# A fifteenth pair of chunks by seven products in the second layer's up-projection

## The chip, the cores and the metric

The kernel runs on one core of one Trainium2 chip. The core has a matrix engine (PE, with its weight loads listed apart as PEld), a vector engine (DVE), a scalar or activation engine (ACT), GpSimd (POOL), and a sync engine (SP) that here only issues transfers. Transfers can also be issued from the queues of ACT and POOL. All of them are served by the core's 16 DMA engines. The metric is the device time of one execution in microseconds (us); before the change it is 1697.43 us, the median of three runs (1696.9 to 1697.5).

## What is computed

Two sequences of 512 tokens, 1024 wide, go through a trunk of two layers in float32. Layer 0 mixes tokens with a Fourier transform, layer 1 with grouped-query attention; each layer then has an MLP with a squared ReLU, and a final norm ends it. What matters here is the MLP of layer 1:

```python
def sq_relu_mlp(h, w_up, w_down):
    a = jnp.maximum(h @ w_up, 0)      # 1024 -> 4096
    return (a * a) @ w_down           # 4096 -> 1024

x = x + sq_relu_mlp(rms_norm(x, mlp_norm[i]), mlp_w_up[i], mlp_w_down[i])
```

The change touches the first product, `h @ w_up`, for layer 1.

## The kernel before

**Number format.** Every operand of a product is split into two float32r halves, high and low, and one product of a 128x128 block of weights with a 128x512 block of activations is three matmuls: high by high, high by low, low by high (`product`, L863). A split is one cast on ACT (L82) and one subtraction on DVE (L83).

**Chunks and pairs.** The 4096 columns of `w_up` are 32 chunks of 128 columns. An ordinary chunk of one sequence takes 8 blocks of the inner dimension by 3 matmuls, which is 24 matmuls, and both sequences take 48. Most chunks are instead taken in pairs. A pair is two chunks, two sequences and two halves of the inner dimension, a product of 2x2 blocks, and it is computed with seven block products in place of eight (a scheme of Strassen and Winograd's kind). A block product is 4 inner blocks by 3 matmuls, 12 matmuls. So a pair takes 84 matmuls, and the same four chunk results done ordinarily take 96. Layer 0 has 16 pairs. Layer 1 has 14 pairs (chunks 0 to 27) and four ordinary chunks (28 to 31); `NPS` holds the two numbers.

**Operands.** `Blocks` makes the activation operands: b11 and b21 from the first sequence, b12 and b22 from the second, and the sums t1 to t4 of them. Each is four slots of the pool `act` (38 slots of 4 KB per partition, tag u4). The second sequence's operands and the sums are made by the generator `second` (L226, eleven steps), which is advanced step by step while the first sequence's products run. b12 is used by ordinary chunks alone.

**Leading pairs.** The products with b11 and b21 of the first `AHEADS[l]` pairs are made ahead, since these operands are there first: 8 pairs in layer 0, 6 in layer 1. A leading pair keeps a slot `t` with these two results until its remaining five products are made, and its weights are read a second time then (`load_sums`, L909). The ordinary chunks of the second sequence, `Regular(1, f)`, follow the leading pairs (L1064), between steps of `second`.

**The rest of each pair.** `rest` (L943) makes the remaining products in the order t2, t3, (for a pair that didn't lead: b21), t1, t4, b22, adds them up on DVE (L947, L951, L960, L969, L978), squares on ACT (L884, L885), and prepares the next pair's weight sums and splits between them. `out` (L982) then forms the sums that the second product needs as its operands, with four subtractions (L986 to L989, on POOL; for the last pair on DVE), and stores seven blocks of 256 KB to memory: three through the ACT queue (`spill_b`), four through SP (`spill_t`).

**The end of the stage.** While the last pair runs, the generator `ahead` (L1247) fetches and splits the first operands of the second product: b11, b21, t1, t3 during the pair, then t2, b22, t4, the first weights `w_row` and `w_sum`, and residuals from `park`. After the last pair come the ordinary chunks of the first sequence, `Regular(0, f)` (`last`, L1079 and L1113), and then the second product's first row (`Row`, weight `w`), and its sums (`Sums`, t1, t3, then t2, b22, t4). An ordinary chunk's result goes to `plain` through the ACT queue (L1008); the last MLP stage at the end of the kernel reads the four plain chunks back.

**Order.** A planner places the instructions of each engine, by its own estimate of times, in the order of the program's priorities. A `with tc.manual_schedule(...)` block keeps the named engines in program order. A slot is taken when its first writer is placed, and whoever takes it waits for the last reader of what it held. The pool of raw weights `rawp` has 5 buffers, that of split weights `wp` has 4, `tmp` 8.

```python
        for r in last:
            r.go()
```

Of the kernel before, what the change touches and what calls it, by code (L numbers as in the profile page):

```python
# [29 lines left out]
EPS = 1e-6  # L30
GRID_W = 64
ROPE_THETA = 10000.0
AHEADS = (8, 6)
NPS = (16, 14)
ROW, SUM = ("b11", "b21"), ("b22", "t1", "t2", "t3", "t4")
ROW_GROUPS = ((0, 4), (4, 4), (8, 4), (12, 4)), ((0, 4), (4, 4), (8, 4), (12, 2))
# [4 lines left out]
def trunk_kernel(ctx, tc, x_in, xt_in, y_out, dcos, dsin, feat, rope, gfour, gcol, grow, gfin,  # L41
                 w_four, w_nyq, w_qkv, w_o, w_up, w_row2, w_row4, w_sum2, w_sum4, w_down):
    nc = tc.nc
# [20 lines left out]
    def tm(shape=(P, 512), dt=F32):  # L64
        return tmp.tile(list(shape), dt, tag="t2", name=nm("t"))
# [4 lines left out]
    def ps():  # L70
        return psp.tile([P, 512], F32, tag="ps", name=nm("ps"))
# [30 lines left out]
    def halves(raw, n=512, home=own):  # L102
        hi, lo = home()
        split(hi[:, : 2 * n], lo[:, : 2 * n], raw)
        return [(hi[:, i * n : (i + 1) * n], lo[:, i * n : (i + 1) * n]) for i in range(2)]
# [740 lines left out]
    def project(q, fo, ws, parts, n=512):  # L846

        o, fs, x = ps(), slice(fo * P, (fo + 1) * P), xt(q, fo)
        for k in range(len(parts)):
# [10 lines left out]
    plain = [[drm.tile([P, 2, 512], F32, name=f"plain_{l}_{f}") for f in range(NF - 2 * NPS[l])]  # L860
             for l in range(2)]

    def product(o, w, h, first=True):  # L863

        n = len(h)
        for k in range(n):
            sl = slice(k * P, (k + 1) * P)
            for i, (x, y) in enumerate(((0, 0), (0, 1), (1, 0))):
                nc.tensor.matmul(o, w[x][:, sl], h[k][y], start=first and k + i == 0,  # L869
                                 stop=k == n - 1 and i == 2, skip_group_check=not first)  # L870

    def first_product(l, blocks, rows, ahead):
        def b(name):
            return [(h[0][:, i], h[1][:, i]) for h in blocks.b[name] for i in range(2)]

        def put(op, p, src, queue):
            for g, (p0, n) in enumerate(ROW_GROUPS[l] if op in ROW else SUM_GROUPS[l]):
                if p0 <= p < p0 + n:
                    (nc.scalar if op in ("b11", "b21", "b22") else queue).dma_start(spill[l][op][g][p - p0], src)

        np_, ah = NPS[l], AHEADS[l]

        def squares(t, src):
            nc.scalar.activation(t, src, AF.Relu)  # L884
            nc.scalar.activation(t, t, AF.Square)  # L885

        class Pair:
# [94 lines left out]
            def out(self, b11, b12, b21, b22, eng=nc.gpsimd, queue=nc.sync):  # L982
# [7 lines left out]
                for op, x in (("b11", b11), ("b21", b21), ("b22", b22), ("t1", t[:, 0]), ("t2", t[:, 1]),  # L990
                              ("t3", b12), ("t4", t4)):
                    put(op, p, x, queue)

        class Regular:


# [6 lines left out]
            def go(self):  # L1003
                q, w, o, t = self.q, halves(self.raw), ps(), tm()
                product(o, w[0], b("b11" if q == 0 else "b12"))
                product(o, w[1], b("b21" if q == 0 else "b22"), False)
                squares(t, o)
                nc.scalar.dma_start(plain[l][self.f - 2 * np_][:, q], t)  # L1008

            def run(self):  # L1010
                self.load()
# [3 lines left out]
        pairs = [Pair(p) for p in range(np_)]  # L1015
# [63 lines left out]
        last = [Regular(0, f) for f in range(2 * np_, NF)]  # L1079
        ahead = ahead(last[1:])  # L1080

        def early(ahead):

            pairs[-1].first()
            pairs[-1].second()
            pairs[-1].late = False
            for _ in range(3):
                yield next(ahead)

        for p, pair in enumerate(pairs[:-1]):  # L1090
            if p >= ah:
                pair.first()
            with tc.manual_schedule(engines={ET.DVE}) if p <= ah else nullcontext():
                done = pair.rest(pairs[p + 1], early(ahead) if not last and p == np_ - 2 else iter(()))
# [12 lines left out]
        with tc.manual_schedule(engines={ET.DVE, ET.SP} | (set() if last else {ET.PE})):  # L1107
            done = pairs[-1].rest(None, ahead)
        with tc.manual_schedule(engines={ET.SP}):
            for _ in ahead:  # L1110
                pass
            pairs[-1].out(*done, nc.vector)
        for r in last:  # L1113
            r.go()

    def second_product(l, blocks, rows, late=lambda split_them: None, ready=lambda m: None):
# [3 lines left out]
        def fetch(op, g, n):  # L1120

            h = []
            for k in range(0, n, 2):
                hi, lo = slot([P, 2, 512], F32R), slot([P, 2, 512], F32R)
                nc.sync.dma_start(f32(lo), spill[l][op][g][k : k + 2].rearrange("n p f -> p n f"))
                h.append((hi, lo))
            return h

        def put(op, h):
            for hi, lo in h:  # L1130
                split(hi, lo, f32(lo))
            b[op] = b.get(op, []) + [(hi[:, i], lo[:, i]) for hi, lo in h for i in range(2)]
# [11 lines left out]
        def residual(q, m):  # L1144
            if (q, m) not in there:
                xs[q, m] = slot([P, 2, 512], F32)
                nc.sync.dma_start(xs[q, m], park[q, m])
                there.add((q, m))
            return xs[q, m]
# [3 lines left out]
        def row_raw(m, g, n):  # L1153
            if (0, m, g) in early:
                return early[0, m, g]
            return load_raw(w_row4[4 * l + g, m] if n == 4 else w_row2[m], (P, 2, n * P))

        def sums_raw(m, g, n):
            if (1, m, g) in early:
                return early[1, m, g]  # L1160
            w = w_sum4[3 * l + g, m] if n == 4 else w_sum2[m]
            return [load_raw(w[:, i : i + 2], (P, 2, n * P)) for i in (0, 2)]
# [78 lines left out]
        def group(i, g, n, ops=(0, 5)):  # L1241
            ops = (("b11", "b21"), ("t1", "t3", "t2", "b22", "t4"))[i][slice(*ops)]
            for op in ops:
                b.pop(op, None)
                put(op, fetch(op, g, n))

        def ahead(regular):  # L1247
            n = SUM_GROUPS[l][0][1]
            if not regular:
                h = fetch("b11", 0, 4)  # L1250
                yield
                put("b11", h)
                h = fetch("b21", 0, 4)
                raws = [row_raw(0, 0, 4)]
                yield
                raws.append(row_raw(1, 0, 4))
                h1 = fetch("t1", 0, n)
                yield
                residual(0, 0)
                h3 = fetch("t3", 0, n)  # L1260
                yield
                put("b21", h)
                rows_early[0] = halves(raws[0], 4 * P)
                yield
                put("t1", h1)
                rows_early[1] = halves(raws[1], 4 * P)
                yield
                for m in range(2, 4):
                    early[0, m, 0] = row_raw(m, 0, 4)
                    residual(0, m - 1)  # L1270
                there_later.append(("t3", h3))
                for op in ("t2", "b22", "t4"):
                    there_later.append((op, fetch(op, 0, n)))
                    if op == "t2":
                        residual(0, 3)
                        early[1, 0, 0] = sums_raw(0, 0, n)
                residual(1, 0)
                return
            group(0, 0, ROW_GROUPS[l][0][1], (0, 1))
            regular[0].load()  # L1280
            yield
            group(0, 0, ROW_GROUPS[l][0][1], (1, 2))
            regular[1].load()
            yield
            group(1, 0, n, (0, 2))
            regular[2].load()
            yield
            group(1, 0, n, (2, 5))
            early[0, 0, 0] = row_raw(0, 0, ROW_GROUPS[l][0][1])
            for q in range(NSEQ):  # L1290
                residual(q, 0)
            early[1, 0, 0] = sums_raw(0, 0, n)
            for q in range(NSEQ):
                residual(q, 1)

        def finish(m):
            left[m] -= 1
            if left[m] == 0:
                nc.vector.tensor_add(xs[0, m][:, 1], xs[0, m][:, 1], e[m])
                nc.vector.tensor_add(xs[1, m], xs[1, m], e[m].unsqueeze(1).broadcast_to([P, 2, 512]))  # L1300
                ready(m)

        first_product(l, blocks, rows, ahead)
        e += [tm() for _ in range(4)]
        items, waiting = [], []
# [308 lines left out]
    for n in range(1, len(heads) + 1):  # L1614
        pts, nxt = [], []
        for t in range(NT):
# [3 lines left out]
            if n in (3, 5, 7, 9) and t == 0:  # L1620
                i = (n - 3) // 2
                rotate(raw[:, i * 256 : (i + 1) * 256].rearrange("p (h d) -> p h d", h=2), rt["q"], 2 + i // 2,
                       [late[i]], nc.gpsimd)
        last = nxt[-1] if nxt else last
# [8 lines left out]
        for i in {6: (0, 1), 8: (2,), 10: (3,)}.get(n, ()):  # L1633
            x = late[i].rearrange("p (h d) -> p h d", h=2)
# [94 lines left out]
    with tc.manual_schedule(engines={ET.PE, ET.Activation, ET.DVE, ET.Pool, ET.SP}):  # L1729
# [16 lines left out]
        x = xtok[0]  # L1746
# [196 lines left out]
```

## Time and profile before

| | |
|---|---|
| median of three runs | 1697.43 us |
| the profiled execution, its own time | 1697.05 us |
| its span, first to last instruction | 1695.3 us |
| granted TensorE clock | 0.999 |
| PE busy, matmuls | 1681.1 us, 7845 |
| DVE busy | 1231.3 us |
| ACT busy | 854.8 us |
| POOL busy | 334.6 us |
| leading pairs of layer 1's first product begin | about 1062 us |
| last pair of it ends, second product begins | 1350.64 us, about 1372.4 us |

The profile is one execution, with every instruction's start and duration, and what released it when its engine had been idle. A matmul's listed duration (about 390 ns) is longer than the distance to the next one, because matmuls overlap; lengths of PE work are therefore read from the start of one stretch to the start of the next. The profiled execution's own time is 1.75 us above its span and 0.38 us below the median.

### The profile page before, as it was taken

How to read it: one execution, taken by the hardware profiler on the slowest of the kernel's cores; microseconds unless marked ns; L12 is line 12 of the kernel's file. 1: busy time of each engine (PE TensorE's matmuls, PEld its weight loads, DVE VectorE, ACT ScalarE, POOL GpSimd, SP SyncE). 2: the span in 40 equal slices, each digit the busy share in tenths (PEclk: the TensorE clock that was granted, in tenths of full speed). 3: DMA queues.
4: the chain of work that ended last, by engine and by line, in shares of the span. 5: the costliest groups of instructions: out<-in, count | busy, mean ns of one | idle time of the engine just before them, and what ended most of it. 6: DMA issues, size and time to landing. Idle time of an engine off the chain costs nothing. (4 is left out here: it accounts for less than half of the span.)

```text
span 1695.3 us, 21868 instructions
## 1 busy us (share of the span) xinstructions
PE 1681.1 (99%) x7845; PEld 1395.1 (82%) x7845; DVE 1231.3 (73%) x1808; ACT 854.8 (50%) x1489; POOL 334.6 (20%) x304
## 2 busy tenths in 40 slices
PE   9999999999999999999999999999999999999998
PEld 7987888888788888888888888788888888888887
DVE  8788776557887879886588744687655479787864
ACT  7566444446243434467787714654444544344334
POOL 1321443221000000132344303014422200000002
PEclk9999999999999999999999999999999999999999
DMA  9643555449454545511000213335544686455322
GB/s 341 165 149 111 198 188 180 156 167 386 179 199 145 211 146 181 211 57 38 26 26 1 100 60 127 104 122 197 181 143 154 226 301 238 157 211 185 131 75 100
DMA packets 103679, 265.81 MB, mean 157 GB/s; under 512 B 10177, under 2 KB 10177, under 8 KB 103570
## 3 DMA queue, kind: packets, MB, share of 16 engines
q1 hardware_dynamic: 87266, 232.43, 39.0%
q10 hardware_dynamic: 14400, 26.22, 4.1%
q0 software_dynamic: 1904, 5.77, 1.7%
q8 instruction: 61, 1.00, 0.2%
q14 instruction: 48, 0.39, 0.1%
HBM read 189.40 MB, written 73.92 MB: 155 GB/s over the span
## 5 line engine op out<-in xcount | busy, mean ns | idle before, releaser
L869 PE MATMUL ps<-u,w 128*128 128x512 f32 x4656 | 1065.7, 389 | 3.4 <-DVE w L83 2.5
L869 PEld LDWEIGHTS ps<-u,w 128*128 128x128 f32 x4656 | 872.6, 188 | 187.9 <-DVE w L83 4.2
L82 ACT CAST w<-raw 128x1024 fp32r<-128x1024 f32 (+1 forms) x224 | 217.6, 981 | 442.3 <-PE ps L869 256.5
L83 DVE TENSOR_TENSOR w<-raw,w 128x1024 fp32r<-128x1024 f32 (+1 forms) x224 | 255.1, 1142 | 57.3 <-ACT w L82 56.7
L156 POOL TENSOR_TENSOR t<-t,t 128x512 f32<-128x512 f32 (+1 forms) x56 | 77.8, 1389 | 738.9 <-ACT t L154 683.0
L83 DVE TENSOR_TENSOR u<-u,u 128x1024 fp32r<-128x1024 f32 (+1 forms) x131 | 156.2, 1220 | 23.9 <-ACT u L82 23.3
L82 ACT CAST u<-u 128x1024 fp32r<-128x1024 f32 (+1 forms) x131 | 131.3, 1044 | 74.8 <-PE ps L869 47.8
L77 PE MATMUL ps<-u,u 128*128 128x512 f32 (+2 forms) x388 | 150.2, 388 | 0.4 <-DVE u L83 0.4
L1135 DVE TENSOR_TENSOR u<-ps,u 128x512 f32<-128x512 f32 x160 | 109.5, 686 | 53.5 <-PE ps L869 53.0
L79 PE MATMUL ps<-u,u 128*128 128x512 f32 (+2 forms) x388 | 144.4, 372 | 0.0
L78 PE MATMUL ps<-u,u 128*128 128x512 f32 (+2 forms) x388 | 144.2, 372 | 0.0
L869 PE MATMUL ps<-u,u 128*128 128x512 f32 x576 | 137.9, 390 | 0.6 <-DVE t L960 0.5
L869 PEld LDWEIGHTS ps<-u,u 128*128 128x128 f32 x576 | 107.8, 188 | 24.5 <-issue 0.9
L986 POOL TENSOR_TENSOR u<-u 128x512 f32<-128x512 f32 x28 | 37.2, 1328 | 401.0 <-ACT u L885 401.0
L83 DVE TENSOR_TENSOR u<-ps,u 128x512 fp32r<-128x512 f32 (+4 forms) x118 | 74.8, 650 | 19.5 <-ACT u L82 18.4
L79 PEld LDWEIGHTS ps<-u,u 128*128 128x128 f32 x388 | 73.1, 189 | 13.0
L77 PEld LDWEIGHTS ps<-u,u 128*128 128x128 f32 x388 | 73.3, 189 | 10.8 <-DVE u L83 0.6
L78 PEld LDWEIGHTS ps<-u,u 128*128 128x128 f32 x388 | 73.4, 189 | 10.4
L947 DVE TENSOR_TENSOR t<-ps,u 128x512 f32<-128x512 f32 x30 | 20.7, 691 | 80.6 <-PE ps L869 58.5
L82 ACT CAST u<-ps 128x512 fp32r<-128x512 f32 (+4 forms) x118 | 65.5, 561 | 27.3 <-PE ps L79 11.7
L852 DVE TENSOR_TENSOR u<-ps,u 128x512 f32<-128x512 f32 (+1 forms) x48 | 30.9, 644 | 64.4 <-PE ps L79 64.4
L77 PE MATMUL ps<-u,w 128*128 128x512 f32 (+2 forms) x192 | 65.0, 339 | 0.0
(247 smaller groups left out, 1986.9 us busy)
## 6 DMA issues: line engine op xcount, KB each, us to landing
raw<-w_up SPq DMA_DIRECT2D x82, 512.0 KB, 4.5
u<-spill_t SPq DMA_DIRECT2D x60, 512.0 KB, 6.2
raw<-w_sum SPq DMA_DIRECT2D x56, 512.0 KB, 4.1
u<-spill_b SPq DMA_DIRECT2D x45, 512.0 KB, 5.2
spill_t<-u SPq DMA_DIRECT2D x87, 256.0 KB, 2.0
spill_b<-t ACTq DMA_DIRECT2D x60, 256.0 KB, 3.1
raw<-w_row SPq DMA_DIRECT2D x28, 512.0 KB, 3.9
park<-u SPq DMA_DIRECT2D x24, 512.0 KB, 3.4
```

The costliest lines, as they stand in the source:

```text
L77: nc.tensor.matmul(out, lh, rh, start=first, stop=False)
L78: nc.tensor.matmul(out, lh, rl, start=False, stop=False)
L79: nc.tensor.matmul(out, ll, rh, start=False, stop=last)
L82: nc.scalar.copy(dst_hi, src)
L83: eng.tensor_sub(dst_lo, src, f32(dst_hi))
L156: nc.gpsimd.tensor_add(acc[q][:, :n], acc[q][:, :n], s[:, :n])
L852: nc.vector.tensor_add(x[:, :n], o[:, :n], x[:, :n])
L869: nc.tensor.matmul(o, w[x][:, sl], h[k][y], start=first and k + i == 0, stop=k == n - 1 and i == 2, skip_group_check=not first)
L947: nc.vector.tensor_add(u2, ob, t[:, 0])
L986: eng.tensor_sub(t[:, 0], b12, b11)
L1135: nc.vector.tensor_add(x, o, x)
```

## The change

`NPS[1]` stays 14 and sizes what the second product takes as pairs; the number of pairs of the first product is now `NPS[l] + l`, 15 in layer 1. The fifteenth pair is chunks 28 and 29; ordinary chunks are left for 30 and 31. The fifteenth pair is the last one and its results are stored plain, as the ordinary chunks were: four stores of 256 KB through SP, no subtractions. Pair 13, which was last, now goes through the ordinary `out` on POOL. In layer 1 eight pairs lead. `Regular` runs 2 chunks for each sequence in place of 4, and the steps of `second` that stood between four of them now stand between the two more leading pairs. In `ahead` two loads for ordinary chunks that no longer exist are gone.

```diff
-AHEADS = (8, 6)
+AHEADS = (8, 8)
 NPS = (16, 14)
...
-        np_, ah = NPS[l], AHEADS[l]
+        np_, ah = NPS[l] + l, AHEADS[l]
...
+            def out_plain(self, b11, b12, b21, b22):
+                for i, x in enumerate(((b11, b12), (b21, b22))):
+                    for q in range(2):
+                        nc.sync.dma_start(plain[l][i][:, q], x[q])
...
-                nc.scalar.dma_start(plain[l][self.f - 2 * np_][:, q], t)
+                nc.scalar.dma_start(plain[l][self.f - 2 * NPS[l]][:, q], t)
...
-            pairs[-1].out(*done, nc.vector)
+            if last:
+                pairs[-1].out_plain(*done)
+            else:
+                pairs[-1].out(*done, nc.vector)
...
             group(0, 0, ROW_GROUPS[l][0][1], (1, 2))
-            regular[1].load()
             yield
             group(1, 0, n, (0, 2))
-            regular[2].load()
             yield
```

## The prediction

> **What bounds the kernel now.** I read the page first, then the waits of PE, then the chain of waits, to see whether matmuls taken away shorten the span one for one.
>
> ```profile
> span 1695.3 us, 21868 instructions
> PE 1681.1 (99%) x7845; PEld 1395.1 (82%) x7845; DVE 1231.3 (73%) x1808; ACT 854.8 (50%) x1489; POOL 334.6 (20%) x304
> ...
> PE ps L869 <- DVE w L83: 2.5, 2, 1.5
> PE ps L356 <- POOL u L334: 1.8, 1, 1.8
> PE ps L869 <- DVE u L224: 0.9, 1, 0.9
> ...
> 1081.07 294.22 PE ps L869 x1296
> 1375.28 0.03 issue
> 1375.31 14.17 PE ps L869 x60
> ```
>
> The first two lines are the page's: PE is busy 99% of the span. The next three are the longest waits of PE (total, times, longest). The last three, from the chain of waits, are layer 1's first product from its second pair on: 1296 matmuls run without a gap from 1081.07 to 1375.28, that is 294.22 / 1296 = 0.227 us each. The only wait of PE in the touched stage is the 0.9 us before it is under way. So PE is the bound here, and it has nothing left to lose but matmuls: a matmul removed is worth 0.227 us as long as everything else still arrives in time, and anything late is a loss of its own.
>
> **What goes.** Before: 14 pairs of 84 matmuls and 8 ordinary products of 24, 1368. After: 15 of 84 and 4 of 24, 1356. Twelve fewer: 12 x 0.227 = **2.72 us**. All other engines are asked whether they keep up, in the two places where the cover changes. Let T be the start of pair 0's remaining products and E the end of the last pair.
>
> **The start, up to T.** The leading products are 6 x 24 + 4 x 24 = 240 matmuls before and 8 x 24 + 2 x 24 = 240 after, so T stays. The splits of weights are 10 either way, and the weight loads of the stage are 42 either way (two more second readings and two more for the pair, four fewer for ordinary chunks). b12 and b22 are needed first by an ordinary chunk: two leading pairs later, 48 matmuls or 10.9 us of ease. What is tight is DVE and, newly, the slots:
>
> ```profile
> 1100.00:1117.00 17.00, 17.00 (x77) 14.08 (x76) 16.84 (x17) 11.22 (x15) 0.00 (x0) 1.00 0.23 81
> 1117.00:1131.00 14.00, 14.00 (x63) 11.59 (x62) 12.22 (x16) 8.34 (x12) 0.00 (x0) 1.00 0.34 114
> ...
> 1116.84 1.22 DVE L83 TENSOR_TENSOR u<-u,u 128x1024 fp32r<-128x1024 f32 x1
> ...
> 1120.92 2.36 DVE L83 TENSOR_TENSOR u<-u,u 128x1024 fp32r<-128x1024 f32 x2
> ...
> 1127.60 2.88 PE L869 MATMUL ps<-u,u 128*128 128x512 f32 x12
> ```
>
> The first two rows are windows: length, then busy us of PE, PEld, DVE, ACT and POOL with their counts, the clock, the DMA engines' share and GB/s. DVE is busy 16.84 us of 17. The other rows are from the timelines. At 1127.60 pair 0 begins its b22 product (its weights are u tiles); four products of 12 x 0.227 lie ahead of it, so T = 1127.60 - 10.88 = 1116.72. The last two splits, t4, end at 1123.28, and the t4 product starts at T + 8.16 = 1124.88: 1.6 us to spare. After the change eight `t` slots are held, not six. Counting slots with the sums made as early as in this trace: b11, b21, b12, b22 and t2 hold 20, unsplit t1, t3, t4 six, the `t` eight, 34 of 38. Then t3 brings it to 36, half of t1 to 37, and the second half of t1 finds one slot and waits for b12, which is read last 2.72 us ahead of T. t1 is needed at T + 5.44, t4 at T + 8.16; three splits of 1.22 us after one cast of about 1 us from T - 2.72 end near T + 2. The bad end: all six splits and both sums wait for b12 and DVE does pair 0's own additions between them, 1.04 + 8 x 1.14 + 5 x 0.69 = 13.6 us from T - 2.72, which is 2.7 us after the t4 product's time. **Between 0 and 2.7 us; I take 0**, by the row of DVE at 1116.84, where a half of t1 is split at T already.
>
> **Between T and E.** Eight pairs have 60 matmuls left in place of six, seven have 84 in place of eight. Layer 0 already leads with eight, with seven operands of four slots and no b12, the same filling of the pool:
>
> ```profile
> 236.20 2.88 PE L869 MATMUL ps<-u,u 128*128 128x512 f32 x12
> 238.92 11.04 PE L869 MATMUL ps<-u,w 128*128 128x512 f32 x48
> 249.80 5.60 PE L869 MATMUL ps<-u,u 128*128 128x512 f32 x24
> 255.24 5.60 PE L869 MATMUL ps<-u,w 128*128 128x512 f32 x24
> ...
> 1131.00:1145.00 14.00, 14.00 (x63) 11.62 (x62) 10.66 (x13) 6.19 (x9) 6.33 (x4) 1.00 0.54 190
> ```
>
> These PE rows are layer 0's step from pairs that led to pairs that didn't (its first weights are lent slots, u): each stretch starts where the one before ends. In a short pair DVE is busy 10.66 us of 14 and the transfers 0.54. I cost this stretch at nothing, covered by PE. Pair 13's subtractions go from DVE to POOL,
>
> ```profile
> L986 POOL TENSOR_TENSOR u<-u x13: 1291/1294/2083, 1132.8 to 1334.1; 128x512 f32<-128x512 f32 x13
> L986 DVE TENSOR_TENSOR u<-u x1: 685/685/685, 1363.6 to 1363.6; 128x512 f32<-128x512 f32 x1
> ```
>
> 4 x 1.29 = 5.2 us of POOL, idle 80% of the span, and 4 x 0.69 = 2.7 us less DVE at the end. The added pair's 9 vector operations of 0.69 us lie within its 19 us.
>
> **The end, from E.** Here 96 matmuls (21.8 us) covered the fetching and splitting for the second product; now it is 48 (10.9 us). What they cover:
>
> ```profile
> 1350.64 24.64 PE L869 MATMUL ps<-u,w 128*128 128x512 f32 x108
> ...
> 1352.10 0.36 SPq L1125 DMA_DIRECT2D u<-spill_b  x1
> 1352.55 0.42 SPq L1125 DMA_DIRECT2D u<-spill_t  x1
> 1353.02 0.46 SPq L91 DMA_DIRECT2D raw<-w_row  x1
> 1354.69 1.03 SPq L1147 DMA_DIRECT2D u<-park  x2
> 1360.06 1.68 SPq L91 DMA_DIRECT2D raw<-w_sum  x2
> ...
> 1362.45 1.22 DVE L83 TENSOR_TENSOR w<-raw,w 128x1024 fp32r<-128x1024 f32 x1
> 1365.36 0.43 DVE L1202 TENSOR_TENSOR raw<-raw,raw 128x256 f32<-128x256 f32 x1 [1.09 <-DMA raw<-w_sum]
> 1367.51 0.42 DVE L1203 TENSOR_TENSOR raw<-raw,raw 128x256 f32<-128x256 f32 x1
> 1375.29 1.63 DVE L83 TENSOR_TENSOR u<-raw,u 128x512 fp32r<-128x512 f32 x3 [6.57 <-ACT u L82]
> ```
>
> E is 1350.64. The first row's weights are split by 1363.67 = E + 13.0; after the change they are needed at E + 10.9. The weights of its sums have landed by 1365.36 = E + 14.7, and need two sums, a cast and a split, some 2.2 us; they are needed at E + 10.9 + 2.7 = E + 13.6. So at unchanged times both are late: what counts is how much earlier the transfers get through.
>
> ```profile
> 1338.00:1342.00 4.00, 4.00 (x19) 3.33 (x18) 1.93 (x3) 0.00 (x0) 1.27 (x2) 1.00 0.70 226
> 1354.00:1358.00 4.00, 4.00 (x19) 3.30 (x19) 3.25 (x4) 2.91 (x4) 0.00 (x0) 1.00 1.06 408
> 1366.00:1370.00 4.00, 4.00 (x19) 3.30 (x19) 2.69 (x6) 0.60 (x1) 0.00 (x0) 1.00 1.03 399
> 1370.00:1374.00 4.00, 4.00 (x20) 3.30 (x19) 0.00 (x0) 1.40 (x3) 0.00 (x0) 1.00 0.55 182
> ...
> SPq L91 <- DMA spill_b<-t: 4.3, 1, 4.3
> SPq L1125 <- DMA spill_b<-u: 4.2, 1, 4.2
> ...
> 1339.71 0.39 SPq L1125 DMA_DIRECT2D u<-spill_b  x1
> ```
>
> The DMA engines are full, at about 400 GB/s, until 1370, and SP waited twice for the last pair's own stores (4.2 and 4.3 us). From 1339.71 = E - 10.9 to the landing of `w_sum` SP issues 12 transfers of 512 KB, two of `park` and two halves, with three stores of 256 KB from ACT: 16.5 x 0.524 MB = 8.6 MB, 21.6 us at 400 GB/s; it took 25 us, 3.6 us more. After the change two chunk loads are gone from that list and the three stores too (the plain ones stand behind the `park` loads in SP's order): 13 x 0.524 = 6.8 MB, 17.0 us, so `w_sum` lands between E + 6.1 and E + 9.7 and is split between E + 8.3 and E + 11.9, ahead of E + 13.6. By the same count `w_row`, 3 x 0.524 MB = 3.9 us less, lands 3.9 us earlier, is split at E + 9.1 and needed at E + 10.9. It fits, with some 1.7 us to spare. A cast placed behind the last ordinary chunk's squares on ACT already made the first sums' product a little late (12 matmuls in 3.29 us in place of 2.88, the split above at 1375.29); that 0.4 us stays in any case. For other small lateness I take **0.4 us** more; the bounds are 0 and, at unchanged times with DVE's 2.7 us of subtractions gone, E + 17.0 against E + 13.6, 3.4 us.
>
> [...]
>
> **Sum.** -2.72 + 0 + 0 + 0.4 = -2.3 us. On the profiled execution's own 1697.05 (its span and 1.75 us around it) that is 1694.7; the median stands 0.38 higher, so the forecast is **1695.1 us**, 0.14% below 1697.43. A measurement of this kernel can tell about 0.2%, 3.4 us, from no change, so this counts as no change.
>
> **Rivals**, in time of the median.
> - *The start is late*: a wait of PE for DVE's t1 or t4 split in pair 0, 0.5 to 2.7 us, leaves 0 to -2.2: 1695.2 to 1697.4, most likely 1696.4. For it: DVE at 16.84 of 17 us and a pool now filled to the last slot. Against it: 1.6 us to spare, and layer 0. Chance 0.17.
> - *The second product starts as late behind the last pair as before*, because SP again waits for some store: 3.4 us, or 5.0 if DVE is not freed in time, less 2.72. That is +0.7 to +2.3, **slower than before**: 1698.1 to 1699.7. It decides from `w_sum` landing later than E + 13.6 - 2.2 + 2.7 = E + 14.1. For it: the two rows of SP's waits. Against it: their stores have left. Chance 0.13.
> - *The whole queue of transfers must drain first*: full until 1370 = E + 19.4, less two loads (2.6 us) E + 16.8, plus 2.2 us of sums and splits: 5.4 us late, and the following sums' weights, next in the queue, up to 2 us more: +2.7 to +4.7, 1700.1 to 1702.1. Chance 0.06.
> - *More is gained than the matmuls*: the 0.9 us wait at the start and the 0.4 us at the end vanish too: -4.0, 1693.4. Only with another order by the planner. Chance 0.04.
>
> The forecast holds with 0.60, at 1694.3 to 1696.0. The range of 8 in 10 reaches over the first rival and part of the second: **1694.0 to 1699.0**. Faster by over 0.2% (below 1694.0) has 0.06, slower by over 0.2% (above 1700.8) 0.05, within it 0.89.
>
> **What would show it.** 12 matmuls fewer (7833); the same T; PE stretches of 0.227 us per matmul from T to E, which comes 480 + 588 - 1032 = 36 matmuls or 8.2 us later; 48 matmuls between E and the first row; the DMA share falling within some 12 us of E. A wait of PE on a u tile's split near 1117 to 1125 shows the first rival, on L83 near E + 11 to E + 14 the second and third. The forecast is wrong if PE waits more than 1.3 us in all in these two places, or if the planner's new order costs PE a wait elsewhere.

## The result, and the profile after

| | before | after |
|---|---|---|
| median | 1697.16 us (1696.72 to 1697.50, 4 runs) | 1715.8 us (1715.50 to 1716.04, 4 runs) |
| ratio, 95% interval | | 1.0107 [1.0095, 1.0118] |
| span of the profiled execution | 1695.3 us | 1714.3 us |
| granted TensorE clock | 0.999 | 0.995 |

The change made the kernel 18.6 us slower. The forecast was 1695.1 us with 1694.0 to 1699.0 as its range, so it was wrong, by far more than the range allowed. The page of the kernel after:

```profile
span 1714.3 us, 21868 instructions
PE 1686.6 (98%) x7833; PEld 1396.0 (81%) x7833; DVE 1238.1 (72%) x1813; ACT 856.2 (50%) x1490; POOL 342.6 (20%) x308
```

The 12 matmuls are gone (7833 for 7845), and yet PE is busy 5.5 us longer. So time was lost in two ways: PE stood still, and some matmuls ran slower. The longest waits of PE after (total, times, longest):

```profile
PE ps L869 <- DVE w L83: 5.3, 4, 2.6
PE ps L869 <- ACT w L82: 4.5, 1, 4.5
PE ps L869 <- DVE t L951: 3.4, 1, 3.4
PE ps L869 <- ACT u L82: 2.0, 2, 1.2
...
PE ps L869 <- DVE u L83: 1.0, 1, 1.0
```

Before, the touched stage had one wait, of 0.9 us. Where the new ones lie is seen in the timeline of PE after (start, length, count, and in brackets the wait ahead with what ended it):

```profile
1081.25 38.15 PE L869 MATMUL ps<-u,w 128*128 128x512 f32 x163
1120.16 7.14 PE L869 MATMUL ps<-u,w 128*128 128x512 f32 x29 [0.76 <-ACT u L82]
1130.68 4.57 PE L869 MATMUL ps<-u,w 128*128 128x512 f32 x12 [3.39 <-DVE t L951]
1135.05 2.95 PE L869 MATMUL ps<-u,u 128*128 128x512 f32 x12
...
1366.32 11.04 PE L869 MATMUL ps<-u,w 128*128 128x512 f32 x48
1381.89 1.22 PE L869 MATMUL ps<-u,w 128*128 128x512 f32 x2 [4.54 <-ACT w L82]
1383.34 4.58 PE L869 MATMUL ps<-u,w 128*128 128x512 f32 x10 [0.23 <-DVE w L83]
1389.11 3.29 PE L869 MATMUL ps<-u,u 128*128 128x512 f32 x12 [1.19 <-ACT u L82]
...
1402.06 5.29 PE L869 MATMUL ps<-u,u 128*128 128x512 f32 x22 [1.04 <-DVE u L83]
...
1434.85 5.31 PE L869 MATMUL ps<-u,w 128*128 128x512 f32 x15 [2.58 <-DVE w L83]
```

There are two places, the two that the prediction asked about. In the **lead**, the stretch of 204 matmuls up to pair 0's b22 product takes 1135.05 - 1081.25 = 53.8 us where it took 1127.60 - 1080.82 = 46.8 us: 7.0 us lost, 4.15 of them in the two waits. At the **end**, E is 1366.32; the second product begins at E + 15.6 in place of E + 10.9, and it waits four times more, 9.6 us in all.

The rest of the loss is the clock. Windows of the kernel after, each from about where PE resumes (length, busy us of PE, PEld, DVE, ACT, POOL with counts, granted clock, share of the DMA engines, GB/s):

```profile
1130.60:1134.60 4.00, 3.92 (x11) 3.12 (x12) 2.36 (x3) 3.05 (x4) 0.00 (x0) 0.64 0.02 4
1383.00:1387.00 4.00, 3.77 (x10) 2.88 (x10) 1.81 (x5) 0.00 (x0) 0.00 (x0) 0.50 0.57 214
1434.50:1438.50 4.00, 3.65 (x10) 2.87 (x11) 4.00 (x5) 0.49 (x1) 0.00 (x0) 0.63 0.89 326
```

After each of the three long waits (3.39, 4.54 and 2.58 us) the granted clock is 0.50 to 0.64 for some 4 us, and the ten matmuls from 1383.34 on take 4.58 us, twice 0.227 each. In the windows of 4 us that follow on these three it is 0.93, 0.91 and 0.95.

The account of the span, +19.0 us: 0.5 that already stands ahead of the stage (its first product after the 0.9 us wait starts at 1062.74, not 1062.28), 7.0 in the lead, -2.7 for the twelve matmuls, and the remaining 14.2 from E on, 9.6 of it waits. Of the 4.6 us that are left, about 4 are clock: the ten matmuls from 1383.34 and the fifteen from 1434.85 take 9.9 us where 25 x 0.227 would be 5.7. The 0.5 us lies within what executions differ by: a stretch of 24 matmuls behind it starts at 1074.88 before and at 1075.31 after, and in the profiles of the kernels below anywhere from 1074.72 (fifteen pairs, six leading) to 1075.88 (fourteen pairs, eight leading).

### The profile page after: what moved, and what is told of

Read it like the earlier page. It is cut to its first block, busy times and chain, and to the rows that moved or that the text cites. A ratio compares the mean times of both kernels' runs of the same rounds, so it can differ in the third digit from the quotient of the medians.

```text
span 1714.3 us, 21868 instructions
## 1 busy us (share of the span) xinstructions
PE 1686.6 (98%) x7833; PEld 1396.0 (81%) x7833; DVE 1238.1 (72%) x1813; ACT 856.2 (50%) x1490; POOL 342.6 (20%) x308
## 5 line engine op out<-in xcount | busy, mean ns | idle before, releaser
L83 DVE TENSOR_TENSOR u<-ps,u 128x512 fp32r<-128x512 f32 (+4 forms) x118 | 74.7, 649 | 19.6 <-ACT u L82 18.5
```

Of the source, the lines that this page charges most:

```text
L83: eng.tensor_sub(dst_lo, src, f32(dst_hi))
```

## Two causes, as the traces suggest them

**The lead.** In layer 1 one step of `second` is taken per leading pair from pair 4 on. A step's slots are taken in program order, so its casts come behind that leading pair's own copy (L903). Before, with six leading pairs, the steps after pair 5 had no such pair ahead of them. ScalarE's timeline before:

```profile
1092.82 0.58 ACT L903 COPY u<-ps 128x512 f32<-128x512 f32 x1
...
1093.28 2.95 ACT L82 CAST u<-u 128x1024 fp32r<-128x1024 f32 x3
```

and after:

```profile
1093.23 0.58 ACT L903 COPY u<-ps 128x512 f32<-128x512 f32 x1
...
1093.70 1.05 ACT L82 CAST u<-u 128x1024 fp32r<-128x1024 f32 x1
...
1098.92 0.58 ACT L903 COPY u<-ps 128x512 f32<-128x512 f32 x1
...
1099.39 1.05 ACT L82 CAST u<-u 128x1024 fp32r<-128x1024 f32 x1
...
1104.61 0.58 ACT L903 COPY u<-ps 128x512 f32<-128x512 f32 x1
...
1105.07 1.05 ACT L82 CAST u<-u 128x1024 fp32r<-128x1024 f32 x1
```

Three casts in a row have become one per leading pair, 5.7 us apart. The sums that need them (L240 is the first of t1) start 9.5 us later. The line L240 before, with its first and last start:

```profile
L240 DVE TENSOR_TENSOR u<-u,u x2: 1218/1218/1218, 1097.8 to 1104.8; 128x1024 f32<-128x1024 f32 x2
```

and after:

```profile
L240 DVE TENSOR_TENSOR u<-u,u x2: 1217/1218/1220, 1107.3 to 1113.1; 128x1024 f32<-128x1024 f32 x2
```

From there on DVE has no pause (windows after):

```profile
1110.00:1120.00 10.00, 9.40 (x42) 7.45 (x40) 10.00 (x10) 5.69 (x8) 0.00 (x0) 1.00 0.14 52
1120.00:1130.00 10.00, 7.14 (x29) 5.29 (x29) 9.97 (x12) 5.48 (x7) 0.00 (x0) 1.00 0.38 131
```

**The end.** The first row's weights had landed in time: the load of `w_row`, issued at 1363.83, took 9.3 us (issue table after: KB, us to landing).

```profile
raw<-w_row SPq DMA_DIRECT2D x1, 512.0 KB, 9.3
```

That is E + 6.8, and PE wants the split at E + 10.9. But ScalarE's timeline after reads

```profile
1377.39 0.60 ACT L884 ACTIVATE t<-ps 128x512 f32<-128x512 f32 x1 [1.67 <-PE ps L869]
1377.89 1.04 ACT L82 CAST u<-u 128x1024 fp32r<-128x1024 f32 x1
...
1379.85 1.04 ACT L82 CAST u<-u 128x1024 fp32r<-128x1024 f32 x1 [0.40 <-ACT t L885]
1380.80 1.04 ACT L82 CAST w<-raw 128x1024 fp32r<-128x1024 f32 x1
```

while before it read

```profile
1359.09 2.00 ACT L82 CAST u<-u 128x1024 fp32r<-128x1024 f32 x2
1360.99 1.05 ACT L82 CAST w<-raw 128x1024 fp32r<-128x1024 f32 x1
1361.93 1.07 ACT L884 ACTIVATE t<-ps 128x512 f32<-128x512 f32 x2
```

The order is turned round. The cast of the row's weights, and two casts of operands, now stand behind the squares (L884) of the last ordinary chunk. Those can only start when PE has finished that chunk, which is the moment at which PE itself wants the weights. The wait of 1.19 us one product later looks the same: the casts for the first sums stand behind the copy that ends the first row (L1147), which waits for PE. ScalarE's timeline after:

```profile
1387.96 0.59 ACT L1147 COPY t<-ps 128x512 f32<-128x512 f32 x1 [6.12 <-PE ps L869]
1388.44 1.45 ACT L82 CAST u<-raw 128x512 fp32r<-128x512 f32 x3
```

A second suspect was SP: it waited 5.9 and 8.7 us for plain stores (waits of SP's queue after).

```profile
SPq L91 <- DMA plain<-t: 8.7, 1, 8.7
...
SPq L997 <- DMA plain<-t: 5.9, 1, 5.9
```

## The experiments

All ratios are to the kernel before, with 95% intervals. They were measured in three groups, each with the kernel before beside it: its median was 1697.1 us beside the two steps, the six leading pairs, the first sequence's plain stores and the row's split; 1697.6 us beside the kernel before with eight leading pairs, all final plain stores, the cover given back and all cures; 1697.7 us beside the last two. The changed kernel's 1715.8 us was measured beside 1697.2, so differences between groups carry some 0.5 us.

### Two steps per leading pair

```diff
-                for _ in range(3 - 2 * l):
+                for _ in range(2 * (p < 7) if l else 3):
```

> The changed kernel, but leading pairs 4, 5 and 6 advance the operand generator by two steps each and pair 7 by none (in the changed kernel each of 4 to 7 advances it by one). Theory A (steps pinned): slots are taken in program order, so each step's first cast cannot be placed before the first copy of the leading pair that stands ahead of it; one step for each pair leaves DVE idle about 9 us before T, and the work that is left over makes PE wait 0.76 and 3.39 us at pair 0 with about 2.8 us more at a reduced clock. Then here these two waits go and the time falls by 5 to 7 us from 1715.8, to about 1709 to 1711; the waits at the end of the stage stay. Rival B (slots): eight held result slots leave too few for t1, t3 and t4 until b12 is read. Then taking the steps earlier fills the pool earlier and nothing is gained: 1714 to 1718, with the wait near 1120 to 1130 still there.

Measured: 1709.54 us, 1.0072 [1.0057, 1.0087], 6.3 us below the changed kernel. PE's timeline has one stretch:

```profile
1081.55 47.64 PE L869 MATMUL ps<-u,w 128*128 128x512 f32 x204
```

Both waits in the lead are gone, and the waits of the end are what they were (4.5, 1.2, 1.0 and 2.6 us). The eight leading pairs hold their slots of the pool `act` as in the changed kernel, so it was not the size of the pool that made the steps late.

### Fifteen pairs, six of them leading

```diff
-AHEADS = (8, 8)
+AHEADS = (8, 6)
```

> The changed kernel, fifteen pairs, but six leading pairs as before the change. Leading work is 192 matmuls in place of 240, so the remaining products of pair 0 begin 10.9 us earlier. Theory A: the steps run as early as before the change, yet DVE (busy 16.8 of 17 us in that stretch before the change) has 10.9 us less for them; PE waits some 6 to 9 us at pair 0, most of it at full or half clock, and the whole is at or above the changed kernel: 1714 to 1722. Rival B (slots): with six held slots nothing waits for slots, PE waits 0 to 3 us at pair 0, and the time falls to about 1708 to 1711. Both: the end of the stage loses what it loses in the changed kernel (about 14 us with what follows in the second product).

Measured: 1715.73 us, 1.0111 [1.0094, 1.0128]. The lead loses as much as with eight, in another way: the steps come as early as before (L240 at 1097.6), but 48 matmuls fewer stand ahead of pair 0's b22 product, which begins at 1123.72, 43.1 us after the stretch's start at 1080.65 in place of 156 x 0.227 = 35.4 us. Its listed waits are 3.1 us (1.50, 0.45, 0.41, 0.74), and the granted clock from 1100 to 1120 is 0.83. Right behind the first three waits, which lie within four microseconds with one matmul between each two, 28 matmuls take 9.29 us (from 1110.84) where 28 x 0.227 would be 6.4.

### The kernel before with eight leading pairs

Fourteen pairs and four ordinary chunks, `AHEADS = (8, 8)`, nothing else.

> The kernel before (fourteen pairs, four ordinary chunks) with eight leading pairs instead of six, nothing else. Pinned-steps theory: the steps still stand one behind each of the pairs 4 to 7, so they come as late as in the changed kernel, and the lead loses as it does there in place of T's matmuls: DVE t and ACT u waits of 2 to 6 us, 1699 to 1705. Rival (it is the number of pairs, not the lead, that makes the lead late): no wait in the lead, 1696.5 to 1697.5. In both, no 4.5 us wait before the second product.

Measured: 1697.83 us, 1.0 [0.9991, 1.001]. The first theory of this expectation falls as it was put: the steps are as late as in the changed kernel, and still nothing waits. PE's timeline of this kernel, and the line L240:

```profile
1081.82 58.24 PE L869 MATMUL ps<-u,w 128*128 128x512 f32 x252
```

```profile
L240 DVE TENSOR_TENSOR u<-u,u x2: 1219/1220/1221, 1107.8 to 1113.6; 128x1024 f32<-128x1024 f32 x2
```

I had overlooked that with four ordinary chunks two more leading pairs also mean 48 more matmuls before pair 0 needs its sums. What decides is the time between the first t1 sum and pair 0's b22 product. Worked out for each kernel as matmuls x 0.227 less the start of L240 (both from the stretch's first matmul), beside what the stretch really took:

| kernel | matmuls | first L240 after | time left then | stretch without waits | stretch taken |
|---|---|---|---|---|---|
| before | 204 | 17.0 us | 29.3 us | 46.3 us | 46.8 us |
| changed | 204 | 26.0 us | 20.3 us | 46.3 us | 53.8 us |
| two steps per pair | 204 | 18.4 us | 27.9 us | 46.3 us | 47.5 us |
| 15 pairs, 6 lead | 156 | 17.0 us | 18.5 us | 35.4 us | 43.1 us |
| 14 pairs, 8 lead | 252 | 26.0 us | 31.2 us | 57.2 us | 58.1 us |

With 27.9 us or more the lead loses no more than 1.2 us; with 20.3 and 18.5 us it loses 7.5 and 7.7, so that b22 is reached 27.8 and 26.1 us after the first sum. So the chain of sums, casts and splits seems to need about that long; this is worked out from the table, not measured by itself. The changed kernel took both ends of the slack: fifteen pairs leave two ordinary chunks fewer as cover, and two more leading pairs, with a step pinned to each, use the time that they give back.

### The first sequence's plain stores on POOL's queue

```diff
-                nc.scalar.dma_start(plain[l][self.f - 2 * NPS[l]][:, q], t)
+                (nc.scalar if q else nc.gpsimd).dma_start(plain[l][self.f - 2 * NPS[l]][:, q], t)
```

The line issues the stores of chunks 30 and 31 for the first sequence, two in all.

> The changed kernel, but the plain stores of the first sequence's two ordinary chunks are issued from POOL's queue, not ACT's. Theory C (order on ACT): the first row's weights are cast only behind the squares of the last ordinary chunk, which wait for PE, so the wait of 4.5 us (and the clock lost after it) stays; only the second half of the first sums' weights, which stood behind the landing of one such store for 8.7 us, comes earlier, and 1 to 3 us are gained: 1713 to 1715. Theory D (order of transfers): this hold of SP's queue is what makes the second product late; then the waits from 4.5 us on vanish or halve and 8 to 12 us are gained: 1704 to 1708. If transfers are limited by bandwidth alone, nothing changes: 1715 to 1717.

Measured: 1714.07 us, 1.01 [1.0085, 1.0115], 1.7 us below the changed kernel. The long wait shrinks from 4.54 to 3.23 us and the others stay (1.19, 1.04, 2.58). Without the issues of the stores between squares and casts (0.33 us each in the changed kernel) ScalarE is through a little sooner: PE, which waits for the row's cast, resumes at 1380.14, E + 14.3, in place of E + 15.6. With all final plain stores on POOL's queue, further down, SP's queue waits for no plain store any more (5.9 and 8.7 us in the changed kernel), and yet this wait is 3.23 us there too. So that hold was not what made the second product late.

### The row's split ahead of the last squares

The split of row 0 is issued inside `ahead`, as soon as its load is, the split of the ordinary chunks' weights ahead of all, and ScalarE keeps program order there:

```diff
+            rows_early[0] = halves(early[0, 0, 0], 4 * P)
...
-        with tc.manual_schedule(engines={ET.SP}):
+        for r in last:
+            r.prep()
+        with tc.manual_schedule(engines={ET.SP} | ({ET.Activation} if last else set())):
...
-        for r in last:
-            r.go()
+            for r in last:
+                r.go()
```

> The changed kernel with ACT held in program order at the end of the stage: the weights of the two last ordinary chunks are split first, then the operands t2, b22, t4 and the first row's weights (split here, not in the second product), and the squares of the ordinary chunks come behind them. The stores stay where they were. Theory C (order on ACT): the first row's weights landed 6.8 us behind the last pair's end and are split by some 9 us behind it, so the wait of 4.5 us before the second product goes, and with it the 10 matmuls at half clock: 5 to 8 us gained, 1708 to 1711. Theory D (order of transfers): the first sums' weights still land late and PE waits 3 to 5 us one product later, so at most 2 us are gained: 1714 to 1716.

Measured: 1709.58 us, 1.0073 [1.0058, 1.0088], 6.2 us below the changed kernel. ScalarE's timeline of this kernel:

```profile
1375.93 1.04 ACT L82 CAST w<-raw 128x1024 fp32r<-128x1024 f32 x1
1376.88 0.58 ACT L884 ACTIVATE t<-ps 128x512 f32<-128x512 f32 x1
```

and PE's:

```profile
1378.65 2.56 PE L869 MATMUL ps<-u,w 128*128 128x512 f32 x10 [0.90 <-DVE w L83]
```

No transfer was taken away, only orders were changed, ScalarE's above all, and of the 4.54 us 0.90 is left; the ten matmuls take 2.56 us, not 4.58. So the long wait was order, not transfer. The waits further in (1.19, 1.04, 2.57) stay.

### All final plain stores on POOL's queue

Both kinds of plain store are issued by POOL (the line of `Regular` as above, and L997 with `nc.gpsimd`). These are the six stores at the end of the stage; the expectation's "eight" counts the second sequence's two, which stay on the ACT queue and are issued long before.

> The changed kernel with all eight last plain stores on the POOL queue and no change of order. If the 1.0 and 2.6 us waits later in the second product are the loads that SP issues late because it stands behind the plain stores' transfers (5.9 and 8.7 us in the changed kernel), both go, and with 1.7 us that the first ordinary chunk's store alone gave: 1709 to 1713. If they stem from the late start of the second product's splits on ScalarE and VectorE, only the 1.7 us come again: 1713 to 1715.

Measured: 1711.75 us, 1.0082 [1.0065, 1.0099], 4.1 us below the changed kernel. The 4.54 us wait is 3.23 us, as with the first sequence's stores alone; the 1.04 us wait goes, the 2.58 us one only falls to 2.0, and 1.19 stays. So the stores on SP's queue may cost some 2 to 3 us beyond those of ScalarE's; the two intervals overlap, so the size of it is not shown. The last wait has another cause.

### The cover given back

The products of the last ordinary chunks of the first sequence are made twice, which leaves the output as it is:

```diff
-                product(o, w[0], b("b11" if q == 0 else "b12"))
-                product(o, w[1], b("b21" if q == 0 else "b22"), False)
+                for _ in range(2 - q):
+                    product(o, w[0], b("b11" if q == 0 else "b12"))
+                    product(o, w[1], b("b21" if q == 0 else "b22"), False)
```

The expectation's "48 more matmuls" is the sum over both chunks, 24 for each.

> The changed kernel in which the first product of each of the two last ordinary chunks is made twice over, so that 48 more matmuls (10.9 us) stand before each and the output is the same. Cover theory: waits before and in the second product (4.5, 1.2, 1.0, 2.6 us) and the half clock go, some 9 to 14 us, against 10.9 us of added work: 1712 to 1718. Order theory alone: the 4.5 us wait stays nearly whole, since the split still stands behind the squares of the last ordinary chunk, and only the later waits go: 1718 to 1724.

Measured: 1715.84 us, 1.0108 [1.0092, 1.0123], as long as the changed kernel: 48 matmuls more, 10.9 us, and 10.9 us of waits and slow clock less. PE's timeline of this kernel:

```profile
1365.72 24.64 PE L869 MATMUL ps<-u,w 128*128 128x512 f32 x108
...
1434.18 26.20 PE L869 MATMUL ps<-u,w 128*128 128x512 f32 x108 [2.57 <-DVE w L83]
```

With 96 matmuls behind E, as before the change, the first waits of the end (4.54, 0.23, 1.19 and 1.04 us) are gone. This does not separate cover from order, as I had wanted, because the planner also put the casts ahead of the last squares again; the kernel with all cures, next, does separate them. But the last wait, 2.57 us, stays with all the cover given back.

### All cures together

Two steps per leading pair, all plain stores on POOL, ScalarE's order at the end, and the casts of the first sums ahead of the copy that ends the first row.

> The changed kernel with both cures together and two more of the same kind: two steps of the second product's loads, sums and splits per leading pair; the ordinary chunk's split ahead of the last ordinary chunk's squares on ScalarE; all eight last plain stores on the POOL queue, so that no transfer of SP's waits for one of them; and the casts of the second product's first sums ahead of the copy that ends its first row group. Order theory (every wait of the changed kernel is one of instruction order, and the half clock follows from the waits): all four waits of the end (4.5, 1.2, 1.0, 2.6 us) and both of the lead go, and the time is that of before less 12 matmuls, 1694.4 us, 1694 to 1698. Rival, cover theory (with two ordinary chunks there are 48 matmuls fewer between the last pair and the second product, so what is cured at its start comes back behind it): the two waits at the start go, but 1.0 and 2.6 us stay or grow and the clock falls there again, 1700 to 1704, about what the two cures give when added (1715.8 - 6.2 - 6.2 = 1703.4).

Measured: 1699.76 us, 1.0012 [1.0003, 1.0021], between the two expectations, and 3.6 us less than the two main cures added. The cover is as small as in the changed kernel, 48 matmuls, and still the waits of 4.54, 1.19 and 1.04 us are gone, but for 0.90 us ahead of the row's second half. So the smaller cover alone did not make them: with the orders and queues mended it is enough. One other wait is left:

```profile
1418.50 41.82 PE L869 MATMUL ps<-u,w 128*128 128x512 f32 x183 [2.42 <-DVE w L83]
```

This is the split of the t3 operand of the fifth set of summed weights. The window of the same kernel ahead of it shows DVE without a pause:

```profile
1410.00:1418.00 8.00, 6.08 (x27) 4.69 (x25) 8.00 (x11) 7.67 (x9) 0.00 (x0) 1.00 0.97 358
```

Before the change this same split was just in time. PE's and DVE's timelines before:

```profile
1411.40 48.96 PE L869 MATMUL ps<-u,w 128*128 128x512 f32 x214
```

```profile
1416.19 1.21 DVE L83 TENSOR_TENSOR w<-raw,w 128x1024 fp32r<-128x1024 f32 x1
```

It ended at 1417.4, and the 26 matmuls ahead of its product ended at 1411.40 + 26 x 0.227 = 1417.3. There was nothing to spare, so PE could be earlier there only if DVE was.

### That split moved ahead, and some work of DVE left out

Both start from the kernel with all cures. In the first the fifth sums' t3 operand is split right behind their t1 and t2 operands:

```diff
-                if k:
+                if k and not (l and k == 4):
                     sums.split_3()
...
                         nsums.split_12()
+                        if l and k == 3:
+                            nsums.split_3()
```

> The version with all cures, and the split of the fifth sums' t3 operand issued right behind that of its t1 and t2 operands, ahead of the t4 operand's (layer 1 alone). In the version with all cures TensorE waits once more, 2.4 us for that split, at a time when VectorE is busy without a gap (10.00 of 10 us). If it is VectorE's order alone, the split comes about 2.4 us earlier (two splits of 1.22 us and one of 0.69 stand behind it now), the wait shrinks to 0 to 1.2 us (the operand's other half is next), and the time is 1699.8 less 1 to 2.4, 1697.3 to 1699. If VectorE's work is the bound there whatever its order, the wait goes over to the u split that is now behind it, and the time stays 1699 to 1700.5.

Measured: 1696.06 us, 0.9991 [0.9982, 0.9999]. PE's timeline of this kernel:

```profile
1372.84 2.54 PE L869 MATMUL ps<-u,w 128*128 128x512 f32 x10 [0.90 <-DVE w L83]
...
1419.06 41.32 PE L869 MATMUL ps<-u,w 128*128 128x512 f32 x181 [0.16 <-DVE t L1150]
```

The wait of 2.42 us has become 0.16, and the time fell by 3.7 us, more than the wait, to below the expected range. The runs of the kernel with all cures lay between 1697.9 and 1700.9 us, and its profiled one was among the shortest. Most of the longer ones show a granted clock of 0.998 over the whole run, the three shortest 0.999, so a slower clock behind the same wait may be the rest; no trace of a longer run is kept. In the second kernel the three sums of weights (`sum_123`) are left out for that set, so its output is another one.

> The version with all cures, in which the three sums of layer 1's fifth set of summed weights (1.8 to 2.1 us of VectorE) are left out, so the output changes. If the last 2.4 us wait is VectorE being full from about 1402 us on, it shrinks by about what is left out, to 0 to 0.7 us, and the time to 1697.5 to 1698.5. If the operand's load or its cast comes too late whatever VectorE does, the wait stays at 2 us or more and the time at 1699 to 1700.5.

Measured: 1696.74 us, 0.9998 [0.9988, 1.0007]. PE's timeline of this kernel:

```profile
1417.11 43.13 PE L869 MATMUL ps<-u,w 128*128 128x512 f32 x189 [1.01 <-DVE w L83]
```

The wait falls by 1.4 us where some 1.8 were left out, less than expected (0 to 0.7 us were to be left). So what the wait ends with is VectorE's work, its amount here and its order in the kernel above, not the load or the cast.

## Why the prediction was wrong

**"What goes" was right.** Twelve matmuls are 2.7 us. The kernel with all cures and the moved split fits it: 1694.5 us of span, 0.8 less than before, with 1.1 us of waits left in the second product and 0.6 us of later start and 0.6 us of longer lead that before does not have. -2.7 + 1.1 + 0.6 + 0.6 = -0.4, and it measures -0.8.

**"Between T and E" was right.** From pair 0's b22 product to E are 1366.32 - 1135.05 = 231.3 us after and 1350.64 - 1127.60 = 223.0 before, 8.2 us more, as worked out. POOL took the subtractions without a wait of PE.

**"The start, up to T" failed.** The sentence that failed is "counting slots with the sums made as early as in this trace". The number of matmuls ahead of T stayed 240 as computed, and the slots were not the trouble. But the steps that make the sums are tied one by one to leading pairs, so with two more of them the sums began 9.5 us later. The slack was read from the old trace (1.6 us), as if the feeding work stood where it had stood. The term was taken at 0, with 2.7 as its bad end; 7.0 came. The rival *The start is late* named the right place and the right engine, and was sized by the wrong cause.

**"The end" failed in its order, more than in its transfers.** `w_row` was to land 3.9 us sooner than before behind E; before, it landed at 1353.02 + 7.1 = E + 9.5 (7.1 us to landing in the issue table), after, at E + 6.8, 2.7 us sooner, early enough for the split at E + 9.1 that I had written down. But the cast began at E + 14.5. The prediction had seen the pattern ("a cast placed behind the last ordinary chunk's squares on ACT") and gave it 0.4 us "in any case". That was its price with 96 matmuls of cover, when only the sums' casts stood there. With 48 the planner set three more casts, the row's among them, behind the same squares, and the price was 4.5 us. "It fits, with some 1.7 us to spare" was a sum over transfers that left out the queue in which the next instruction stands. The rival *The second product starts as late behind the last pair as before* was right in sign and place; it looked for a store that SP waits for. That was a part of it, some 4 us at the most (all final stores on POOL), and 0.7 to 2.3 us was too small. The sum over transfers missed it as well: the second half of `w_sum`, forecast to land by E + 9.7, was issued at 1376.9, when SP's wait of 8.7 us was over, and landed 2.6 us later, at E + 13.2. VectorE came to it only at 1383.20, behind the row's late split, so that this lateness was hidden behind ScalarE's.

**Two terms were missing.** The sum ended with the first row and its sums. It did not ask whether the rows behind them could follow PE 2.7 us sooner; the split at 1416.19 could not. And no step had a price for the clock after a wait: of the 18.6 us about 4 at the end, and about 1.7 in the lead (twelve matmuls in 4.37 us in place of 2.72), are matmuls at a lower clock, not waits.

**Is the idea sound?** With the orders mended it takes 1696.06 us, 1.7 us (0.1%) below the kernel before, of the 2.7 us that twelve matmuls are worth. The interval, 0.9982 to 0.9999, only just leaves out no change. That this time lies in the range of the forecast doesn't bear the forecast out: it was made for a kernel without these changes of order.

What stays open: why the clock falls behind some waits and not behind others, and which of the smaller cures (the sums' casts ahead of the copy, the stores on POOL) the last version could do without; neither was left out of it alone.

## What to carry to other kernels

When cover shrinks, ask of each operand not only when its data lands and how long its split takes, but what stands ahead of the split on its engine, and whether that waits for the work which the split is to feed. When a change moves a unit of work to which other steps are tied, the steps move too: take slack from the new order, not from the old trace. And where a trace shows a lower granted clock behind a wait of the matrix engine, count its cost with the wait's: in the changed kernel (0.64, 0.50 and 0.63 behind the three long waits) that added about 5.7 us to 13.7 us of waits.

## What the runs showed of the hardware

In the changed kernel the granted clock was 0.50 after a wait of 4.54 us, 0.64 after 3.39 us and 0.63 after 2.58 us, while the 2.42 us wait of the kernel with all cures and the 2.02 us wait of the one with all final stores on POOL left 1.00 in the profiled executions. With fifteen pairs and six leading, waits of 1.50, 0.45 and 0.41 us in a row were followed by 28 matmuls in 9.29 us in place of 6.4, and the granted clock from 1100 to 1120 was 0.83.

In the changed kernel SP's load of `w_sum` also waited 8.7 us until a plain store, issued from ACT's queue, had landed, and with all those stores on POOL's queue no load of SP waited for one. The traces show the wait and what ended it; why it was there they don't show.
